# adaLN's row products tied to TensorE's weight chunks, in the recurrence and in the down sweeps

## The chip, the cores and the metric

The kernel runs on one core of a Trainium2 chip. Five engines work side by side, each through its own instructions in order: TensorE (PE; its weight loads are listed as PEld), VectorE (DVE), ScalarE (ACT), GpSimd (POOL) and SyncE (SP), whose queue issues the DMAs here. The metric is the device time of one execution in microseconds, as the median of several runs.

## The reference

One decoder block for 512 tokens of width 2048 in float32. An adaLN vector comes from `c` and modulates every sub-layer: two shifts, two scales, two gates, each 2048 long. Cut to what matters:

```python
c_act = silu(c)                                   # 1 x 2048
mod = c_act @ w_ada + b_ada                       # 1 x 12288
sh1, sc1, gt1, sh2, sc2, gt2 = split(mod, 6)
h = rmsnorm(x, norm1_g) * (1 + sc1) + sh1
p = h @ w_in                                      # 2048 -> 4384
mix = concat(rwkv7(p[:3360]), pool(p[3360:])) @ w_out
x = x + gt1 * mix
h = rmsnorm(x, norm2_g) * (1 + sc2) + sh2
x = x + gt2 * (conv_ffn(h) @ w_down)              # 5632 -> 2048
out = rmsnorm(x, norm_f_g)
```

`rwkv7` is a recurrence over the tokens for 16 heads of width 64; `pool` takes moving means over 2, 4, 8 and 16 tokens.

## The kernel before, in words

Everything is laid out with features on the 128 partitions and the 512 tokens along the free axis. A planner (the tile framework) lays out each engine's order of instructions ahead of time: it takes instructions in the order of their priority (the order in which they are written down, unless a block raises it) as soon as its own clock says that their inputs and buffers are there. On the chip each engine then runs its list strictly in that order and waits on semaphores. Buffers of one tag are handed out in the order in which their tiles are written down.

**Projections.** `project` takes the weights in chunks of 128 x 512 (four 128 x 128 blocks): `split_weights` loads a chunk into `wraw` (four buffers, L113), ScalarE rounds it to `whi` (L115), VectorE takes the rest `wlo` (L117; three buffers each), and `mm3` issues three matmuls a block (L121 to L123), twelve a chunk.

**adaLN's rows.** `mod` has 96 columns of 128 values. Each is a row product: a slice of w_ada is loaded with 128 rows on the partitions, and one VectorE instruction multiplies it by the broadcast `silu(c)` and sums it up (`scalar_tensor_tensor` with `accum_out`, followed by a short read of the accumulator). The first 32 (1024 KB each, L196) are made in the first stage. The next 48 are cut into halves of 1024 elements, 96 rows of 512 KB, in `ada_rest` (L364 to L373, tile `war`, two buffers, broadcast `cq`, results in `modq`). The last 16, the gates of the down projection, are cut into quarters of 512 elements, 64 rows of 256 KB, in `ada_gate2` (L1079 to L1085, tile `wa` under tag t1, broadcast `cb2` under tag t0, two buffers each, results in `modg`).

**The recurrence** (L711 to L742) goes through four groups of four heads. `front` and `rest` of a group are written under a raised priority (`hp`); in `rest` a scan of eight steps (L607 to L636) goes back and forth between TensorE, VectorE (L612, L634) and ScalarE (`ua`, L617). Under groups 0 to 2 the projections of the next group's heads run as filler: `win_some`, six tiles of four chunks, 24 chunks a group. The pool heads are done there too; their weights (`load_pw`, L295) share the two buffers of tag `war` with the rows. `ada_rest(24 * g, 24 * g + 24)` is written at the end of each of groups 0 to 2, at plain priority. Under group 3 and behind it runs most of the output projection, `project(ps, a["wout"][f, :, 0 : NM * P], M)` for ten tiles `f`, 40 chunks (L758 to L767), and `ada_rest(72, 96)` is written behind that (L768). The stage that follows loads x back (L854) and uses `mod[:, 48:80]` in its norm.

**The down sweeps.** `actd` holds 44 tiles of the activated up-projection. The first sweep (L1088 to L1101) goes through them in 11 groups of DK = 4: `act_tiles` loads and splits four (L1064, L143, L144), then `down` runs one weight chunk for each of the NB = 8 output tiles, which sum up in eight banks: 88 chunks. The second sweep (L1104 to L1109) does the other eight output tiles over nine groups, 72 chunks; the last two groups of it are done in token halves behind that. In the first sweep, groups 1 to 8 have eight rows each in front of their chunks:

```python
if 1 <= n <= 8:
    ada_gate2((n - 1) // 2, range(8 * ((n - 1) % 2), 8 * ((n - 1) % 2) + 8))
```

Group 9 adds up the quarters into `mod[:, 80:96]`. The gates are used when the last group of the first sweep goes through `residual`, and in L1109 at the end of the second.

Of the kernel before, what the change touches and what calls it, by code (L numbers as in the profile page):

```python
# [1 line left out]

# [1 line left out]

# [5 lines left out]
F32 = mybir.dt.float32  # L10
# [3 lines left out]
ALU = mybir.AluOpType  # L14
PSUM = bass.MemoryType.PSUM

P = 128
T = 512
D = 2048
KT = D // P  # L20
NF = 44
# [7 lines left out]
NB = 8  # L29
# [5 lines left out]
DK = 4  # L35
# [27 lines left out]
def block_kernel(ctx, tc, a, out, stop=None, dbg=None):  # L63
    nc = tc.nc
    V, S, G, PE = nc.vector, nc.scalar, nc.gpsimd, nc.tensor
# [23 lines left out]
    def cols(name, lo, hi):  # L89
        return vec[:, COLS[name] + lo : COLS[name] + hi]  # L90
# [11 lines left out]
    mod = cp.tile([P, 96], F32, tag="mod", name="mod")  # L102
# [3 lines left out]
    V.tensor_scalar_add(b1p, cols("b_ada", 16, 32), 1.0)  # L106

    mark = [None, None]

    def split_weights(src, eng=V):  # L110
        w = src.shape[-1]
        raw = wp.tile([P, WC], F32, tag="wraw", name="wraw", bufs=4)
        nc.sync.dma_start(raw[:, 0:w], src)  # L113
        hi = wp.tile([P, WC], F32R, tag="whi", name="whi", bufs=3)
        mark[0] = S.copy(hi[:, 0:w], raw[:, 0:w]).ins  # L115
        lo = wp.tile([P, WC], F32R, tag="wlo", name="wlo", bufs=3)
        mark[1] = eng.tensor_tensor(lo[:, 0:w], raw[:, 0:w], hi[:, 0:w].bitcast(F32), op=ALU.subtract).ins  # L117
        return hi, lo

    def mm3(ps, wh, wl, xh, xl, start, stop):  # L120
        PE.matmul(ps, wh, xh, start=start, stop=False)  # L121
        PE.matmul(ps, wh, xl, start=False, stop=False)  # L122
        return PE.matmul(ps, wl, xh, start=False, stop=stop)  # L123

    def project(ps, src, acts, start=True, stop=True, engs=(V,)):

        n = len(acts)
        for k0 in range(0, n, WC // P):
            nk = min(WC // P, n - k0)
            wh, wl = split_weights(src[:, k0 * P : (k0 + nk) * P], engs[k0 // 4 % len(engs)])  # L130
            for kk in range(nk):
                k = k0 + kk
                sl = slice(kk * P, (kk + 1) * P)
                last = mm3(ps, wh[:, sl], wl[:, sl], *acts[k], start=start and k == 0, stop=stop and k == n - 1)
        return last

    def slots(k, tag="a"):
        return (actp.tile([P, T], F32R, tag=f"{tag}h{k}", name=f"{tag}h{k}"),
                actp.tile([P, T], F32R, tag=f"{tag}l{k}", name=f"{tag}l{k}"))
# [32 lines left out]
    cact = tc.dram_tile([1, D], F32, name="cact")  # L172
# [6 lines left out]
    if True:  # L179
        cb = p0.tile([P, D], F32, tag="cb", name="cb")  # L180
# [29 lines left out]
        for k in range(KT):  # L210
# [7 lines left out]
            hi, lo = slots(k)  # L218
# [26 lines left out]
        for k in range(KT):  # L245
# [3 lines left out]
            hi, lo = slots(k)  # L249
# [111 lines left out]
    cq = [None]  # L361
    modq = ra.tile([P, 2, 48], F32, tag="modq", name="modq")

    def ada_rest(n0, n1):  # L364
        for n in range(n0, n1):
            kq, j = divmod(n, 48)
            if j == 0:
                cq[0] = ra.tile([P, 2 * T], F32, tag="cq", name="cq")
                nc.sync.dma_start(cq[0], cact[0:1, kq * 2 * T : (kq + 1) * 2 * T].partition_broadcast(P))
            wa = ra.tile([P, 2 * T], F32, tag="war", name="war", bufs=2)  # L370
            nc.sync.dma_start(wa, a["ada2"][kq, j, :, :])
            V.scalar_tensor_tensor(wa, wa, 1.0, cq[0], op0=ALU.mult, op1=ALU.mult,  # L372
                                   accum_out=modq[:, kq, j : j + 1])  # L373

    def slab(t):
        return t[:, 0 : 2 * T].rearrange("p (x c t) -> p x c t", x=2, c=NK)
# [308 lines left out]
                last_mix.append(split_act(NM + x, two(rs)[:, x, :]))  # L685

    sp, last_mix = {}, []

    def win_some(pairs, which):
        for p, i in [(p, i) for p in pairs for i in which]:  # L690
            ps = win_tile(3 + 3 * p + i)
            t = ra.tile([P, T], F32, tag="spill", name="spill", bufs=2)
            shift(ps, 8 * i + p, t)
            d = tc.dram_tile([P, T], F32, name=f"sp{p}_{i}")
            nc.sync.dma_start(d, t)
            sp[p, i] = d

    def hp():
        return tc.high_priority(offset=100000)

    shift(win_tile(8), 17, two(rkv0[2])[:, 1, :])
    def load_cells(g, names):
        got = []
        for i in names:
            t = cell(RKV[i], RKV[i].lower())
            for x in range(2):
                nc.sync.dma_start(two(t)[:, x, :], sp[2 * g + x, i])
            got.append(t)
        return got

    UNDER = {0: POOLS[0:1], 1: POOLS[1:2], 2: POOLS[2:4]}  # L711
    rkv = rkv0
    with hp():
        fr, norm = front(0, rkv)
    for g in range(NQ):
        pairs = (2 * g + 2, 2 * g + 3)
        with hp():
            quad = rest(g, rkv, fr)
            next(quad)
        if g < NQ - 1:  # L720
            win_some(pairs, (1,))
        with tc.high_priority(offset=50000):
            for gi in UNDER.get(g, ()):
                pool(gi)
        if g < NQ - 1:
            win_some(pairs, (0, 2))
            with tc.high_priority(offset=50000):
                r, k = load_cells(g + 1, (0, 1))
        with hp():
            next(quad)  # L730
        if g < NQ - 1:
            with tc.high_priority(offset=50000):
                fr, norm = front(g + 1, (r, k, None))
        with hp():
            next(quad, None)
            if g < NQ - 1:
                rkv = [r, k] + load_cells(g + 1, (2,))
        if g < NQ - 1:
            ada_rest(24 * g, 24 * g + 24)
        if g == 2:  # L740
            V.tensor_add(mod[:, 32:48], modq[:, 0, 0:16], modq[:, 1, 0:16])
            V.tensor_add(mod[:, 32:48], mod[:, 32:48], cols("b_ada", 32, 48))  # L742
# [15 lines left out]
    for f in range(NW):  # L758
# [7 lines left out]
        nc.sync.dma_start(d, xt[:, f % 2, :])  # L766
        part.append(d)  # L767
    ada_rest(72, 96)  # L768
    V.tensor_add(mod[:, 48:80], modq[:, 0, 16:48], modq[:, 1, 16:48])
    V.tensor_add(mod[:, 48:80], mod[:, 48:80], cols("b_ada", 48, 80))  # L770
# [8 lines left out]
    rb = ctx.enter_context(tc.tile_pool(name="rb", bufs=1, reuse_waits="tile"))  # L779
# [26 lines left out]
    def residual(f, ps, gate, acc, lo, hi, fresh):  # L806

        V.scalar_tensor_tensor(x2[f][:, lo:hi], ps, gate, x2[f][:, lo:hi], op0=ALU.mult, op1=ALU.add)
        sumsq(acc, x2[f][:, lo:hi], lo, hi, fresh)
# [121 lines left out]
    at = 0  # L931
    for j in range(2, NORD):
        tiles = []
        for i in range(2):
            ps = bank()
            last = project(ps, a["wup"][2 * j + i - 4, :, :], H2)
# [78 lines left out]
    for n in range(NST):  # L1015
# [12 lines left out]
        t1, t2, t3, t4 = ([TK[k][i] for k in ks] for i in range(4))  # L1028
# [29 lines left out]
    def gate(f):  # L1058
        return mod[:, 80 + f : 81 + f]

    def act_tiles(k0):
        got = []
        for k in range(k0, k0 + DK):
            t = wp.tile([P, WC], F32, tag="wraw", name="ald", bufs=4)  # L1064
            nc.sync.dma_start(t, actd[k])
            got.append(split_act(k % KT, t))
        return got

    def down(ps, f, k0, n, acts, start, stop):
        project(ps, a["wdn"][f, :, k0 * P : (k0 + n) * P], acts, start=start, stop=stop)  # L1070
# [5 lines left out]

    modg = cp.tile([P, 4, KT], F32, tag="modg", name="modg")

    def ada_gate2(kq, js):  # L1079
        cb = rb.tile([P, T], F32, tag="t0", name="cb2", bufs=2)  # L1080
        nc.sync.dma_start(cb, cact[0:1, kq * T : (kq + 1) * T].partition_broadcast(P))
        for j in js:
            wa = rb.tile([P, T], F32, tag="t1", name="wa3", bufs=2)
            nc.sync.dma_start(wa, a["ada3"][kq, j, :, :])
            V.scalar_tensor_tensor(wa, wa, 1.0, cb, op0=ALU.mult, op1=ALU.mult, accum_out=modg[:, kq, j : j + 1])  # L1085

    pss = [bank() for _ in range(NB)]
    for k0 in range(0, NF, DK):  # L1088
        A = act_tiles(k0)
        n = k0 // DK  # L1090
        if 1 <= n <= 8:
            ada_gate2((n - 1) // 2, range(8 * ((n - 1) % 2), 8 * ((n - 1) % 2) + 8))
        if n == 9:
            V.tensor_add(modg[:, 0, :], modg[:, 0, :], modg[:, 1, :])
            V.tensor_add(modg[:, 2, :], modg[:, 2, :], modg[:, 3, :])
            V.tensor_add(modg[:, 0, :], modg[:, 0, :], modg[:, 2, :])
            V.tensor_add(mod[:, 80:96], modg[:, 0, :], cols("b_ada", 80, 96))
        for f in range(NB):
            down(pss[f], f, k0, DK, A, k0 == 0, k0 + DK == NF)
            if k0 + DK == NF:  # L1100
                residual(f, pss[f], gate(f), acc, 0, T, f == 0)  # L1101
    pss = [bank() for _ in range(NB)]
    KL = NF - 2 * DK
    for k0 in range(0, KL, DK):  # L1104
        A = act_tiles(k0)
        for f in range(NB):
            down(pss[f], NB + f, k0, DK, A, k0 == 0, k0 + DK == KL)
            if k0 + DK == KL:
                V.scalar_tensor_tensor(x2[NB + f], pss[f], gate(NB + f), x2[NB + f], op0=ALU.mult, op1=ALU.add)  # L1109
    A = act_tiles(KL) + act_tiles(KL + DK)  # L1110
    for hf in range(2):
        for n in range(NB):
            f = NB + n
# [121 lines left out]
```

## Time and profile before

| | |
|---|---|
| median of 3 runs | 2365.94 us (2362.83 to 2372.0) |
| the profiled execution | 2367.17 us, its span 2365.4 us |
| granted TensorE clock, mean | 0.979 |
| PE busy | 2224.0 us, 94% |
| PEld busy | 1883.8 us, 80% |
| DVE busy | 1512.8 us, 64% |
| ACT busy | 924.0 us, 39% |
| POOL busy | 404.7 us, 17% |
| the 96 rows of L372 | 117.2 us of DVE, 1222 ns each, first at 196.3 us, last at 738.5 us |
| the 64 rows of L1085 | 43.8 us of DVE, 690 ns each, first at 1860.7 us, last at 2004.6 us |

The span runs from the first to the last instruction; the time of an execution has a little more around it. In a row of a view, a group of instructions has its line, engine, operation, output and inputs, shapes and count; then the busy time and the mean length of one, then the engine's idle time in front of them and what ended it. `DVE war L372 <- DMA war<-ada` in the table of waits means that VectorE stood idle in front of instructions of L372 until the DMA into `war` had landed; the numbers are the total, the count and the longest. A matmul's recorded length overlaps the next one's, so matmuls are best counted by window. Windows give, for each engine, busy time and count, and then the granted TensorE clock (1.00 is full), the mean busy share of the 16 DMA engines and GB/s.

### The profile page before, as it was taken

The numbers are of one execution on the slowest core, as the hardware profiler recorded it, in microseconds if no ns is written. First come the engines' busy times: TensorE is split into PE (matmuls) and PEld (weight loads), VectorE is DVE, ScalarE is ACT, GpSimd is POOL, SyncE is SP. The second block draws the span as 40 slices with busy tenths as digits, with TensorE's granted clock in tenths as the row PEclk, the third lists the DMA queues.
The fourth block names the chain that finished last, engine by engine and source line by source line (L and its number), as shares of the span: only waits on it lengthen the run. The fifth ranks groups of instructions, "written<-read, shape, count | busy, mean of one in ns | idle before, by whom it ended". The sixth has DMA issues, their size and how long they took to land.

```text
span 2365.4 us, 41904 instructions
## 1 busy us (share of the span) xinstructions
PE 2224.0 (94%) x16306; PEld 1883.8 (80%) x16306; DVE 1512.8 (64%) x2532; ACT 924.0 (39%) x1551; POOL 404.7 (17%) x390
## 2 busy tenths in 40 slices
PE   7998888898979899999999999999999998999997
PEld 5776656665656798889999999999999766888886
DVE  7897667576876469766566666665666555353357
ACT  4335233242423255544434444444444322343333
POOL 0000000000000005643443343433342000000000
PEclk9999999999989999999999999999999999999998
DMA  9885555636775575533333333333334877555555
GB/s 349 301 305 170 157 188 164 205 117 206 226 225 163 179 225 169 148 115 109 116 121 115 113 121 108 116 116 113 109 115 133 272 242 231 148 152 143 143 164 179
DMA packets 197466, 401.42 MB, mean 170 GB/s; under 512 B 37521, under 2 KB 49553, under 8 KB 193041
## 3 DMA queue, kind: packets, MB, share of 16 engines
q1 hardware_dynamic: 197266, 398.73, 53.1%
q8 instruction: 128, 2.10, 0.4%
q14 instruction: 72, 0.59, 0.1%
HBM read 364.56 MB, written 34.09 MB: 169 GB/s over the span
## 4 chain that ended last, share of the span: by engine, by line
PE 48%; DMA 5%; DVE 2%; issue 1%; ACT 0%; SPq 0%; DVEq 0%; ACTq 0%
PE b L123 16%; PE b L121 16%; PE b L122 16%; DMA wa<-ada 2%; DMA ald<-actd 2%; DMA wraw<-wdn 1%; DVE wlo L117 1%; DVE wa L1085 0%; DVE x L1074 0%; DMA x<-x2d 0%; ACT ah L143 0%; DVE al L144 0%; ACT whi L115 0%; SPq L1054 0%; PE b L170 0%
## 5 line engine op out<-in xcount | busy, mean ns | idle before, releaser
L115 ACT CAST whi<-wraw 128x512 fp32r<-128x512 f32 (+1 forms) x594 | 360.1, 609 | 827.8 <-DMA wraw<-wup 264.6
L117 DVE TENSOR_TENSOR wlo<-wraw,whi 128x512 fp32r<-128x512 f32 (+1 forms) x578 | 406.0, 705 | 248.3 <-ACT whi L115 239.9
L123 PE MATMUL b<-ah,wlo 128*128 128x512 f32 (+1 forms) x980 | 352.6, 360 | 16.9 <-DVE wlo L117 15.9
L121 PE MATMUL b<-ah,whi 128*128 128x512 f32 (+1 forms) x980 | 351.3, 358 | 9.4 <-ACT whi L115 8.4
L122 PE MATMUL b<-al,whi 128*128 128x512 f32 (+1 forms) x980 | 349.5, 357 | 0.0
L123 PE MATMUL b<-hh,wlo 128*128 128x512 f32 (+1 forms) x640 | 237.4, 371 | 5.5 <-DVE wlo L117 5.4
L121 PE MATMUL b<-hh,whi 128*128 128x512 f32 (+1 forms) x640 | 237.7, 371 | 0.0
L122 PE MATMUL b<-hl,whi 128*128 128x512 f32 (+1 forms) x640 | 237.2, 371 | 0.0
L123 PEld LDWEIGHTS b<-ah,wlo 128*128 128x128 f32 x980 | 186.6, 190 | 53.2 <-DVE wlo L117 26.6
L121 PEld LDWEIGHTS b<-ah,whi 128*128 128x128 f32 x980 | 186.6, 190 | 38.6 <-ACT whi L115 13.7
L122 PEld LDWEIGHTS b<-al,whi 128*128 128x128 f32 x980 | 186.5, 190 | 26.4
L969 DVE TENSOR_TENSOR pl<-raw,ph 128x768 fp32r<-128x768 f32 x104 | 102.9, 989 | 153.6 <-ACT ph L968 153.6
L123 PE MATMUL mm<-ah,wlo 128*128 128x512 f32 x444 | 186.6, 421 | 6.6 <-DVE wlo L117 6.6
L121 PE MATMUL mm<-ah,whi 128*128 128x512 f32 x444 | 185.5, 418 | 7.2 <-ACT whi L115 6.6
L122 PE MATMUL mm<-al,whi 128*128 128x512 f32 x444 | 183.8, 414 | 0.0
L957 POOL TENSOR_TENSOR sums<-sums,raw 128x256 f32<-128x256 f32 x104 | 107.6, 1034 | 416.1 <-DVE sl L969 410.2
L123 PE MATMUL b<-tk,sl 128*128 128x256 f32 x624 | 176.7, 283 | 0.5 <-DVE sl L969 0.5
L122 PE MATMUL b<-tk,sh 128*128 128x256 f32 x624 | 176.6, 283 | 0.0
L121 PE MATMUL b<-tk,sh 128*128 128x256 f32 x624 | 176.1, 282 | 0.0
L372 DVE SCALAR_TENSOR_TENSOR war<-war,cq 128x1024 f32<-128x1024 f32 x96 | 117.2, 1222 | 85.5 <-DMA war<-ada 85.1
L968 ACT CAST ph<-raw 128x768 fp32r<-128x768 f32 x104 | 86.4, 831 | 164.4 <-PE b L122 157.8
L956 POOL TENSOR_TENSOR sums<-raw 128x512 f32<-128x512 f32 x104 | 137.7, 1324 | 67.9 <-DMA raw<-wups 36.3
(277 smaller groups left out, 4711.1 us busy)
## 6 DMA issues: line engine op xcount, KB each, us to landing
raw<-wups SPq DMA_DIRECT2D x104, 512.0 KB, 3.5
war<-ada SPq DMA_DIRECT2D x96, 512.0 KB, 4.3
wraw<-wdn SPq DMA_DIRECT2D x192, 256.0 KB, 3.1
wraw<-wup SPq DMA_DIRECT2D x160, 256.0 KB, 3.6
wa<-ada SPq DMA_DIRECT2D x32, 1024.0 KB, 7.7
wraw<-win SPq DMA_DIRECT2D x108, 256.0 KB, 4.1
ald<-actd SPq DMA_DIRECT2D x88, 256.0 KB, 2.8
wraw<-wout SPq DMA_DIRECT2D x78, 256.0 KB, 4.0
```

The lines of the kernel that those rows point to most:

```text
L115: mark[0] = S.copy(hi[:, 0:w], raw[:, 0:w]).ins
L117: mark[1] = eng.tensor_tensor(lo[:, 0:w], raw[:, 0:w], hi[:, 0:w].bitcast(F32), op=ALU.subtract).ins
L121: PE.matmul(ps, wh, xh, start=start, stop=False)
L122: PE.matmul(ps, wh, xl, start=False, stop=False)
L123: return PE.matmul(ps, wl, xh, start=False, stop=stop)
L372: V.scalar_tensor_tensor(wa, wa, 1.0, cq[0], op0=ALU.mult, op1=ALU.mult, accum_out=modq[:, kq, j : j + 1])
L956: G.tensor_tensor(sa, raw[:, 1:3, :], raw[:, 0:1, :].to_broadcast([P, 2, W2]), op=ALU.add)
L957: G.tensor_tensor(sb2[:, 0, :], sa[:, 0, :], raw[:, 2, :], op=ALU.add)
L968: act = S.copy(hi[:, sl, :], t)
L969: dve = V.tensor_tensor(lo[:, sl, :], t, hi[:, sl, :].bitcast(F32), op=ALU.subtract)
```

## The change

`project` notes the last matmul of each chunk in a list, `beats`. `in_step(op, beat)` tells the planner to place `op` behind that matmul in its order; it is an edge without a semaphore, so nothing waits for it on the chip. In `ada_rest` each row is tied to a beat among those noted since the last call: 24 rows to 24 chunks in groups 0 to 2, and 24 rows to 40 chunks for the last call.

For the gates, `ada_gate2` becomes a generator that issues the loads and keeps one more row loaded than it hands out. `gate_step` is called behind each chunk of both down sweeps and does one row behind every second chunk from the seventh on, tied to that chunk's beat. The rows of the first eight gates come first (32 rows, up to chunk 68), then those of the other eight (up to chunk 132); each half is added up on its own. The row's own instruction, its tiles, its DMAs and their sizes stay as they are. The number of DMAs is the same: 64 rows and eight of `cb2`.

```diff
@@ block_kernel
+    beats = []
+
+    def in_step(op, beat):
+        tc.add_manual_dep(op.ins, beat.name, mybir.DependencyInfo(mybir.DependencyClass.NoSync,
+                                                                  mybir.DependencyReason.DATA), reason="pace")
@@ project
                 last = mm3(ps, wh[:, sl], wl[:, sl], *acts[k], start=start and k == 0, stop=stop and k == n - 1)
+            beats.append(last.ins)
         return last
@@ ada_rest
     def ada_rest(n0, n1):
+        b, at = len(beats) - first_beat[0], first_beat[0]
         for n in range(n0, n1):
...
-            V.scalar_tensor_tensor(wa, wa, 1.0, cq[0], op0=ALU.mult, op1=ALU.mult,
-                                   accum_out=modq[:, kq, j : j + 1])
+            op = V.scalar_tensor_tensor(wa, wa, 1.0, cq[0], op0=ALU.mult, op1=ALU.mult,
+                                        accum_out=modq[:, kq, j : j + 1])
+            i = at + (n - n0) * b // (n1 - n0)
+            if i < len(beats):
+                in_step(op, beats[i])
+        first_beat[0] = len(beats)
@@ ahead of front(0, rkv)
+    first_beat[0] = len(beats)
@@ the gates
-    def ada_gate2(kq, js):
...
+    def ada_gate2(js):
+        loaded = []
+        for kq in range(4):
+            cb = rb.tile([P, T], F32, tag="t0", name="cb2", bufs=2)
+            nc.sync.dma_start(cb, cact[0:1, kq * T : (kq + 1) * T].partition_broadcast(P))
+            for j in js:
+                wa = rb.tile([P, T], F32, tag="t1", name="wa3", bufs=2)
+                nc.sync.dma_start(wa, a["ada3"][kq, j, :, :])
+                loaded.append((wa, cb, modg[:, kq, j : j + 1]))
+                if len(loaded) == 2:
+                    yield loaded.pop(0)
+        yield loaded.pop(0)
+
+    rows = itertools.chain(ada_gate2(range(NB)), ada_gate2(range(NB, KT)))
+
+    def gate_step(n):
+        if n % 2 or n < 6:
+            return
+        row = next(rows, None)
+        if row:
+            wa, cb, got = row
+            in_step(V.scalar_tensor_tensor(wa, wa, 1.0, cb, op0=ALU.mult, op1=ALU.mult, accum_out=got), beats[-1])
+        done = (n - 4) // 2
+        if done in (4 * NB, 4 * KT):
+            lo = done // 4 - NB
...
@@ first sweep
         A = act_tiles(k0)
-        n = k0 // DK
-        if 1 <= n <= 8:
-            ada_gate2((n - 1) // 2, range(8 * ((n - 1) % 2), 8 * ((n - 1) % 2) + 8))
-        if n == 9:
...
         for f in range(NB):
             down(pss[f], f, k0, DK, A, k0 == 0, k0 + DK == NF)
+            gate_step(k0 // DK * NB + f)
@@ second sweep
             down(pss[f], NB + f, k0, DK, A, k0 == 0, k0 + DK == KL)
+            gate_step((NF + k0) // DK * NB + f)
```

More of the change, by code (lines that the diff above doesn't have):

```diff
@@ L1 @@
 from contextlib import ExitStack
+import itertools
 import numpy as np
@@ L687, in block_kernel @@
     sp, last_mix = {}, []
+    first_beat = [0]
     def win_some(pairs, which):
@@ L1077, in block_kernel @@
     modg = cp.tile([P, 4, KT], F32, tag="modg", name="modg")
-    def ada_gate2(kq, js):
[L1080 to L1085, printed above, removed]
+    def ada_gate2(js):
[21 more added lines that the diff above has]
+            lo = done // 4 - NB
+            r = slice(lo, lo + NB)
+            V.tensor_add(modg[:, 0, r], modg[:, 0, r], modg[:, 1, r])
+            V.tensor_add(modg[:, 2, r], modg[:, 2, r], modg[:, 3, r])
+            V.tensor_add(modg[:, 0, r], modg[:, 0, r], modg[:, 2, r])
+            V.tensor_add(mod[:, 80 + lo : 80 + lo + NB], modg[:, 0, r], cols("b_ada", 80 + lo, 80 + lo + NB))
     pss = [bank() for _ in range(NB)]
@@ L1089, in block_kernel @@
         A = act_tiles(k0)
-        n = k0 // DK
-        if 1 <= n <= 8:
-            ada_gate2((n - 1) // 2, range(8 * ((n - 1) % 2), 8 * ((n - 1) % 2) + 8))
-        if n == 9:
[L1094 to L1097, printed above, removed]
         for f in range(NB):
             down(pss[f], f, k0, DK, A, k0 == 0, k0 + DK == NF)
+            gate_step(k0 // DK * NB + f)
             if k0 + DK == NF:
```

## The prediction

> **What bounds the kernel now.** I read the page's part 1 first, then the table of waits, then windows stage by stage, because the rows that the change moves stand in two stages only: the recurrence (196 to 748 us) and the first down sweep (1853 to 2051 us).
>
> ```profile
> PE 2224.0 (94%) x16306; PEld 1883.8 (80%) x16306; DVE 1512.8 (64%) x2532; ACT 924.0 (39%) x1551; POOL 404.7 (17%) x390
> DVE war L372 <- DMA war<-ada: 85.1, 54, 6.2
> DVE wa L1085 <- DMA wa<-ada: 45.1, 38, 3.5
> L372 DVE SCALAR_TENSOR_TENSOR war<-war,cq 128x1024 f32<-128x1024 f32 x96 | 117.2, 1222 | 85.5 <-DMA war<-ada 85.1
> ```
>
> TensorE is busy 94% of the span, so a gain has to come out of its remaining gaps, or out of time in which it issues slowly. The two waits say what adaLN's rows do on VectorE: it stands idle 85.1 us in front of the 96 rows of L372 and 45.1 us in front of the 64 rows of L1085, each time because the row's own DMA has not landed. VectorE takes its instructions in order, so what stands behind such a row waits too. Two short timelines of VectorE show it, first in the recurrence, then in the down sweep:
>
> ```profile
> 427.01 1.23 DVE L372 SCALAR_TENSOR_TENSOR war<-war,cq 128x1024 f32<-128x1024 f32 x1 [6.16 <-DMA war<-ada]
> 428.16 0.08 DVE L372 DVE_READ_ACCUMULATOR war<-war,cq 128x1 f32 x1
> 428.16 1.22 DVE L586 TENSOR_TENSOR X<-X,bt 128x1024 f32<-128x1024 f32 x1
> ...
> 1938.86 0.69 DVE L1085 SCALAR_TENSOR_TENSOR wa<-wa,cb 128x512 f32<-128x512 f32 x1 [3.45 <-DMA wa<-ada]
> 1939.48 0.08 DVE L1085 DVE_READ_ACCUMULATOR wa<-wa,cb 128x1 f32 x1
> 1939.48 0.69 DVE L117 TENSOR_TENSOR wlo<-wraw,whi 128x512 fp32r<-128x512 f32 x1
> ```
>
> At 428.16 the addition to X, on which the recurrence's next matmuls wait, starts in the moment in which a row is done for which VectorE had idled 6.16 us. At 1939.48 it is the split of a weight chunk.
>
> **The down sweeps, term by term.** Windows of equal length, columns busy time and count by engine, then granted clock, DMA share, GB/s: the stretch with the rows, and the one behind it without.
>
> ```profile
> 1877.00:2029.50 152.50, 138.31 (x578) 106.10 (x578) 84.36 (x188) 43.49 (x73) 0.00 (x0) 1.00 0.73 231
> 2029.50:2182.00 152.50, 152.50 (x674) 126.34 (x673) 67.68 (x100) 56.28 (x93) 0.00 (x0) 1.00 0.51 145
> ```
>
> Same kind of matmul, same clock, 578 against 674 in 152.5 us. One takes 152.5 / 674 = 0.2263 us when nothing holds it up, so the 96 that are missing cost 96 x 0.2263 = 21.7 us. That is all the rows can cost there. After the change there is a row (0.69 + 0.08 us of VectorE) per two chunks, which is 2 x 12 x 0.2263 = 5.4 us of TensorE, and VectorE is busy 67.68 of 152.5 us in the rowless stretch; 28 rows more there make it 67.7 + 28 x 0.77 = 89 of 152.5. How long a row's DMA takes stands in the list of DMA issues (size, median time from issue to landing), for the recurrence's rows and for the sweep's:
>
> ```profile
> war<-ada SPq DMA_DIRECT2D x96, 512.0 KB, 4.3
> wa<-ada SPq DMA_DIRECT2D x64, 256.0 KB, 3.6
> ```
>
> In the sweep a row is loaded at least one row ahead, so 5.4 us of lead stand against 3.6 us. The DMAs are as many as before (64 rows, 8 of cb2); 23 of the rows (behind chunks 88 to 132) move into the second sweep, where the DMA share is 0.51 and not 0.73. On SP's queue such an issue still waits for the VectorE row that frees the buffer, with weight loads queued behind it, but these run four buffers ahead. The extra additions (8 of 8 columns instead of 4 of 16) are short, and the gates are due 12 and 20 chunks after them. I take 20 us off, leaving 1.7 us for splits that a row delays. Ends: 21.7 us off if no row is felt; nothing off if the DMAs stay late. If the cover goes, the first to be late is the weight split L117, as now.
>
> **The recurrence.** The four groups end their scans with the eighth `ua` (L617). Windows between the scans, with the first scan and the rest behind the last one (same columns):
>
> ```profile
> 196.00:307.40 111.40, 92.28 (x1052) 68.65 (x1052) 80.17 (x134) 41.87 (x60) 0.95 (x1) 0.91 0.53 159
> 307.40:336.00 28.60, 27.54 (x421) 17.32 (x422) 19.13 (x44) 9.77 (x27) 0.00 (x0) 1.00 0.69 222
> 336.00:441.50 105.50, 88.84 (x1093) 65.53 (x1086) 72.09 (x122) 36.08 (x51) 0.95 (x1) 0.92 0.57 170
> 471.00:568.70 97.70, 88.09 (x1127) 64.08 (x1119) 64.81 (x108) 37.63 (x53) 0.95 (x1) 0.98 0.47 141
> 603.50:716.80 113.30, 92.17 (x1119) 69.26 (x1110) 87.07 (x147) 41.48 (x61) 0.95 (x1) 0.89 0.71 222
> 747.80:813.00 65.20, 64.26 (x356) 51.99 (x345) 24.88 (x39) 19.49 (x35) 0.00 (x0) 1.00 0.38 115
> ```
>
> And VectorE's time in L372 alone, by stretch; a row counts twice there (itself and the read of its sum):
>
> ```profile
> 196.00:307.40 111.40, 22.16 (x36) 0.91 0.53 159
> 307.40:336.00 28.60, 9.84 (x16) 1.00 0.69 222
> 336.00:441.50 105.50, 18.43 (x30) 0.92 0.57 170
> 441.50:471.00 29.50, 8.62 (x14) 1.00 0.63 201
> 471.00:568.70 97.70, 6.99 (x11) 0.98 0.47 141
> 568.70:603.50 34.80, 13.91 (x24) 1.00 0.76 250
> 603.50:716.80 113.30, 27.34 (x45) 0.89 0.71 222
> 716.80:747.80 31.00, 10.61 (x18) 1.00 0.61 191
> ```
>
> What a row costs now. Between the scans, the stretch with 5.5 rows takes 97.7 us and the one with 15 rows 105.5 us: 7.8 / 9.5 = 0.82 us a row. In the scans, two steps without any row give the bare pace:
>
> ```profile
> 464.30:471.00 6.70, 0.00 (x0) 1.00 0.25 79
> 464.41 0.27 ACT L617 COPY ua<-ch 128x128 f32<-128x128 f32 x1 [0.97 <-PE ch L616]
> 471.05 0.27 ACT L617 COPY ua<-ch 128x128 f32<-128x128 f32 x1
> ```
>
> Two steps in 6.64 us, so seven steps need 23.2 us; the four scans take 28.6 + 29.5 + 34.8 + 31.0 = 123.9 us, 31 us more, over 36 rows: 0.86 us a row. With 0.84 us for all 96 the rows cost about 81 us. A row holds VectorE 1.22 + 0.08 us and idles it 85.1 / 96 = 0.89 us more, 2.2 us in all, so some 0.4 of that time lands on the chain.
>
> What the change leaves. Row by row the paces are: 24 weight chunks in each of groups 0 to 2, a row each; 40 chunks of wout for the last 24 rows. A chunk is 12 matmuls, 2.7 us if TensorE does nothing else and about twice that in a group, while a row's DMA lands in 4.3 us, so most rows find their data. One place stays: the rows share the two buffers `war` with the pool weights, in the order in which they are written down. SP's queue shows both pool weights of group 2 taken together and no row until they are free:
>
> ```profile
> 452.35 0.33 SPq L371 DMA_DIRECT2D war<-ada  x1
> 455.94 2.51 SPq L298 DMA_DIRECT2D pw<-poolw  x2
> 548.34 2.89 SPq L371 DMA_DIRECT2D war<-ada  x2
> ```
>
> So group 2's rows cannot begin before 548 us whatever they are tied to, I estimate eight to be overdue by then (a third of the group's 24 chunks), and they run as closely as their DMAs allow, as now. For these and a few others I leave 20 of the 85.1 us of idling. The last group's rows move: now all are done by 748 us, afterwards those whose chunks run behind the scan land in 748 to 813 us, where VectorE is busy 24.88 of 65.2 us, and cost nothing; 64 us of TensorE are some 20 of the 40 chunks, so 10 rows at least. The 86 others cost 0.4 x 1.30 = 0.52 us each, 45 us, and the idling left 0.4 x 20 = 8 us: 53 us against 81, 28 us less. Not all of it is gained. Under group 3's recurrence TensorE has wout to do, and what is not done there is done behind it; of the 15 us that its stretch gives (31 rows at 0.84 against about 20 at 0.52 and a few us of idling) I count half. Gain: 28 - 7 = 21 us.
>
> Ends of this term. The most: TensorE's idle and half-clock time, (window less busy) + busy x (1 - clock), is 27.4, 23.8 and 31.2 us in the windows that start at 196, 336 and 603.5 us and 11.4 in the 97.7 us from 471, where few rows are; brought to that rate the three give 14.4 + 11.5 + 17.9 = 44 us, and the scans at bare pace 31: 75 us. The least lies below zero: the 86 rows each on the chain with their whole 1.30 us are 112 us against 81, 31 us more. I take the middle because few places change where the rows meet the chain, only how long VectorE idles there. The Trainium skill's page "TensorE: Matmul & The Clock Gate" (Part 1: The HAM clock gate) says the array's clock halves after one idle window of about 3.4 us and needs as long to come back; the trace agrees in kind, 0.89 to 0.92 where TensorE idles most, 1.00 in the down sweep where it idles in short pieces. By that rule the windows from 336 and 603.5 us would give 0.06 x 88.8 + 0.09 x 92.2 = 13.6 us from the clock alone if they came to the 0.98 of the one from 471, and the sum would stand at 2311; by the rows it stays, since 0.84 us a row was measured as a whole, clock and all.
>
> The hand-over behind wout: the last rows now end about when the last chunk does. SP's next loads are those of x:
>
> ```profile
> 808.88 0.33 SPq L113 DMA_DIRECT2D wraw<-wout  x1
> 813.22 1.80 SPq L854 DMA_DIRECT2D x<-part  x4
> ```
>
> Chunk 38 of 40 is split before 813 us, its row takes 1.30 us, so these loads aren't held; were rows left over, each would hold them some 2 us (4.3 us of DMA over two buffers). Nothing for it.
>
> **Sum.** The profiled execution took 2367.2 us for a span of 2365.4, and stands 1.2 us above the median of the runs, 2365.9. 2367.2 - 20 - 21 = 2326.2, on the median's footing 2325.
>
> **The rivals.** (a) Only the sweeps pay: the planner puts the rows into the same VectorE gaps of the recurrence, as the group 2 queue shows it must in part: 2365.9 - 20 = 2346. For it: TensorE is busy 27.54 of 28.6 us in a scan already. (b) The recurrence pays far more: rows that find their data hide in VectorE's gaps and cost a third, 27 of 81 us, less 7 in group 3: 47 + 20 off, 2299. For it: the stretch from 471 us, where TensorE loses least, is the one with fewest rows. (c) Slower: a row directly behind a chunk stands just ahead of the next split or the chain's next step, and each of the 86 costs its whole 1.30 us: 31 - 20 gives 2377. It decides from (81 + 20) / 86 = 1.17 us a row. For it: at the start of a group VectorE is full already,
>
> ```profile
> 356.00:376.00 20.00, 15.38 (x237) 12.43 (x240) 19.81 (x25) 8.40 (x13) 0.00 (x0) 1.00 0.59 185
> ```
>
> 19.81 of 20 us with one row in it; against it: there is nearly no idling to add there and the planner ranks rows last. (d) The change doesn't do what it says: the order is laid out by the planner's clock, no wait holds a row behind its chunk on the chip, and the DMAs stay late, 85 and 45 us of idling: 2366. The Trainium skill's "Perfetto Trace Analysis" (Identifying the Most-Contended Engine) would have the engine with the highest occupancy mended first, and by it bubbles on a VectorE at 64% would not move the end; the 96 missing matmuls speak against that.
>
> **How the numbers follow.** Forecast 0.51, (a) 0.22, (b) 0.11, (c) 0.07, (d) 0.09. The forecast's own range is 2308 to 2338. What a measurement can tell from no change is about 0.5%, 12 us. Faster: forecast, (b) and nearly all of (a), 0.82; same: (d) and a little of (a), 0.11; slower 0.07. The range for 8 in 10 takes in (a) and most of (b): 2297 to 2354.
>
> **What would show it.** L1085's successor idles VectorE under 5 us for its DMA, and windows of 152.5 us in the first sweep hold some 670 matmuls. In the recurrence the wait for `war` falls to about 20 us, most of it behind 548 us less the gain, scans take 25 to 27 us, and the last rows stand behind the last scan. Wrong I would be if that wait stays above 50 us, if scans stay at 29 us or more, or if the loads of x wait for a row.

## The result, and the profile after

The changed kernel takes 2332.2 us (median of 5, 2323.1 to 2332.7) where the kernel before takes 2365.9: ratio 0.9836, 95% interval 0.9813 to 0.986. The forecast was 2325 us, with 2308 to 2338 as its own range. The profiled execution took 2332.65 us for a span of 2330.9, against 2365.4 before: 34.5 us.

The page's part 1 of the changed kernel, and from its table of waits the line for the rows of the recurrence (L381 now, L372 before; the last column is the longest wait):

```profile
PE 2202.7 (95%) x16306; PEld 1878.0 (81%) x16306; DVE 1512.6 (65%) x2536; ACT 925.9 (40%) x1551; POOL 403.3 (17%) x390
DVE war L381 <- DMA war<-ada: 47.2, 35, 5.0
```

VectorE does the same work as before and idles 47.2 us in front of the rows instead of 85.1. For the gates' rows (L1115, L1085 before) there is no such line any more: none of the 64 waits for its DMA. The first sweep, in windows of the length used before (busy time and count of PE, PEld, DVE, ACT, POOL; clock, DMA share, GB/s), both now with rows in them:

```profile
1864.00:2016.50 152.50, 152.50 (x675) 126.27 (x674) 74.59 (x142) 51.38 (x84) 0.00 (x0) 1.00 0.66 199
2016.50:2169.00 152.50, 152.50 (x675) 126.27 (x673) 83.59 (x159) 56.37 (x92) 0.00 (x0) 1.00 0.66 199
```

675 matmuls in 152.5 us, where 578 stood beside the rows before and 674 without them: the whole 21.7 us are back. What TensorE lost there before shows in its own waits, here in the window of the 578 (1877 to 2029.5 us):

```profile
PE b L123 <- DVE wlo L117: 11.5, 15, 1.5
```

In the two windows of the changed kernel TensorE waits for no split at all. One place shows why: a row (L1115) now lies between two splits (L124, L117 before) that wait for ScalarE, and costs none of them anything.

```profile
1900.35 0.69 DVE L124 TENSOR_TENSOR wlo<-wraw,whi 128x512 fp32r<-128x512 f32 x1 [2.03 <-ACT whi L122]
1900.96 0.69 DVE L1115 SCALAR_TENSOR_TENSOR wa<-wa,cb 128x512 f32<-128x512 f32 x1
1901.57 0.08 DVE L1115 DVE_READ_ACCUMULATOR wa<-wa,cb 128x1 f32 x1
1903.07 0.69 DVE L124 TENSOR_TENSOR wlo<-wraw,whi 128x512 fp32r<-128x512 f32 x1 [1.42 <-ACT whi L122]
```

The recurrence, in windows cut at the starts and ends of its four scans as before, the last one from the fourth scan's end to the first load of x:

```profile
196.00:299.00 103.00, 85.64 (x1049) 63.88 (x1047) 71.50 (x119) 41.29 (x59) 0.95 (x1) 0.97 0.47 138
299.00:325.20 26.20, 25.38 (x400) 15.74 (x404) 15.13 (x38) 10.24 (x28) 0.00 (x0) 1.00 0.57 181
325.20:428.40 103.20, 87.55 (x1122) 65.05 (x1113) 76.01 (x129) 36.70 (x52) 0.95 (x1) 0.97 0.62 188
428.40:453.50 25.10, 24.68 (x387) 15.19 (x390) 12.82 (x34) 8.93 (x25) 0.00 (x0) 1.00 0.54 173
453.50:561.70 108.20, 93.59 (x1138) 67.48 (x1129) 78.81 (x132) 38.37 (x55) 0.95 (x1) 0.96 0.61 182
561.70:589.70 28.00, 27.69 (x403) 17.23 (x407) 16.98 (x41) 10.34 (x28) 0.00 (x0) 0.93 0.63 193
589.70:696.90 107.20, 86.30 (x1103) 66.55 (x1096) 77.63 (x133) 41.47 (x62) 0.95 (x1) 0.89 0.61 194
696.90:721.70 24.80, 24.57 (x410) 15.31 (x414) 13.45 (x35) 8.72 (x26) 0.00 (x0) 1.00 0.49 143
721.70:798.70 77.00, 74.13 (x378) 60.02 (x371) 46.57 (x79) 21.79 (x39) 0.00 (x0) 1.00 0.68 221
```

The scans take 26.2 + 25.1 + 28.0 + 24.8 = 104.1 us where they took 123.9. Between scans, group 2's stretch became longer, 108.2 against 97.7 us: it was nearly free of rows and now has 16. The third scan ends at 589.7 us (603.5 before, 13.8 us earlier), the fourth at 721.7 (747.8, 26.1 us earlier), and the loads of x, which close the stage, are issued at 798.7 us (813.2, 14.5 us earlier). So the last group won 12.3 us on the chain, and nearly none of it arrived at the loads of x. The two stages' gains, 14.5 and 21.7 us, make up the 34.5 us but for 1.7 us lost between them.

### The profile page after: what moved, and what is told of

It is laid out like the page before. It is cut to its first block, busy times and chain, and to the rows that moved or that the text cites. A ratio compares the mean times of both kernels' runs of the same rounds, so it can differ in the third digit from the quotient of the medians.

```text
span 2330.9 us, 41813 instructions
## 1 busy us (share of the span) xinstructions
PE 2202.7 (95%) x16306; PEld 1878.0 (81%) x16306; DVE 1512.6 (65%) x2536; ACT 925.9 (40%) x1551; POOL 403.3 (17%) x390
## 4 chain that ended last, share of the span: by engine, by line
PE 60%; DVE 2%; DMA 2%; ACT 0%; issue 0%; SPq 0%; DVEq 0%; ACTq 0%
PE b L130 20%; PE b L128 20%; PE b L129 20%; DVE wlo L124 1%; DMA wraw<-wdn 1%; DMA wraw<-wout 1%; DVE hl L159 0%; DVE x L1089 0%; ACT whi L122 0%; DVE acc L819 0%; DMA ald<-actd 0%; DVE h L157 0%; DMA x<-part 0%; DMA x<-x2d 0%; DVE x L823 0%
## 5 line engine op out<-in xcount | busy, mean ns | idle before, releaser
L124 DVE TENSOR_TENSOR wlo<-wraw,whi 128x512 fp32r<-128x512 f32 (+1 forms) x578 | 406.5, 705 | 270.9 <-ACT whi L122 263.1
L381 DVE SCALAR_TENSOR_TENSOR war<-war,cq 128x1024 f32<-128x1024 f32 x96 | 116.9, 1220 | 47.3 <-DMA war<-ada 47.2
```

The source lines that it names most:

```text
L381: op = V.scalar_tensor_tensor(wa, wa, 1.0, cq[0], op0=ALU.mult, op1=ALU.mult, accum_out=modq[:, kq, j : j + 1])
```

## Experiments

The ratios are against the kernel before on the same chip. One measure beside the time is steadier than it: the first load of x, which closes the recurrence's stage with wout. Among four kernels whose recurrence is the same (the changed one and three below) it stands at 794.0, 794.2, 796.5 and 798.7 us, 795.9 in the mean; in the kernel before and one with its recurrence at 813.2 and 816.3, 814.8 in the mean. So one execution's stage is known to some 3 us, and the recurrence's gain is nearer 19 us than the 14.5 us of the one pair of profiles. Every stage time below is that of one profiled execution, which need not be the median one.

| kernel | median us, ratio [95% interval] | fourth scan ends | first load of x | matmuls in 152.5 us, first sweep |
|---|---|---|---|---|
| before | 2365.9 | 747.8 | 813.2 | 578 |
| changed | 2332.2, 0.9836 [0.9813, 0.986] | 721.7 | 798.7 | 675 |
| rec_only | 2348.7, 0.9934 [0.9908, 0.9959] | 714.7 | 794.0 | 581 |
| sweep_only | 2348.2, 0.9931 [0.9904, 0.9958] | 750.9 | 816.3 | 674 |
| no_rows | 2275.8, 0.9632 [0.9605, 0.9659] | 668.9 | 739.6 | |
| rows_nodma | 2302.4, 0.9742 [0.9711, 0.9772] | 691.4 | 766.1 | |
| load_nowait | 2318.6, 0.9791 [0.9771, 0.9812] | 701.7 | 781.4 | |
| own_pw | 2321.3, 0.9804 [0.9783, 0.9824] | 717.4 | 795.3 | |
| shift_late | 2347.9, 0.9927 [0.9898, 0.9955] | 709.6 | 814.2 | |
| shift20 | 2333.8, 0.9866 [0.9847, 0.9886] | 714.5 | 803.0 | |
| shift20_own | 2331.9, 0.9849 [0.9835, 0.9864] | 708.1 | 797.9 | |
| tie_groups | 2336.6, 0.9872 [0.9854, 0.9889] | 730.4 | 800.1 | |
| gate_2per | 2348.8, 0.9922 [0.9902, 0.9943] | 717.6 | 796.5 | 593 |
| gate_1per | 2325.9, 0.9831 [0.9812, 0.9849] | 717.2 | 794.2 | 675 |

### The two parts alone

`rec_only` has the gates' code of before:

```diff
-    def gate_step(n): ...
+        if 1 <= n <= 8:
+            ada_gate2((n - 1) // 2, range(8 * ((n - 1) % 2), 8 * ((n - 1) % 2) + 8))
```

> The changed kernel with the gates' rows put back into the first sweep in bursts of eight; only the recurrence's rows keep their places behind chunks. Theory 1 (the two parts add up, each with its own mechanism): the sweep loses its 21.6 us again, the recurrence keeps its 14.5 us, so about 2332 + 21 = 2353 us, and the end of wout stands at 795 us as in the changed kernel. Rival (the sweep gains because the recurrence now hands over differently): the first sweep keeps some of its gain, below 2345 us.

`sweep_only` has no tie in the recurrence:

```diff
-            if i < len(beats):
-                in_step(op, beats[i])
```

> The changed kernel without the tie of the recurrence's rows to chunks (they are placed as before); only the gates' rows are spread over both sweeps. Theory 1 (the parts add up): 2366 - 21.6 = 2344 us, every group of eight chunks in the sweeps takes 21.76 us. Rival: it needs the other part too, above 2352 us.

2348.7 and 2348.2 us. The ratios multiply to 0.9866, the changed kernel has 0.9836 with an interval that ends at 0.986: within the noise the parts add up. Each stage shows its own part alone, 581 matmuls against 674 in the sweep, 794.0 against 816.3 us for the load of x. `rec_only` ended lower than expected and `sweep_only` higher, by some 4 us each, as their first loads of x do; the sweep itself is as expected.

### What the rows still cost

`no_rows` leaves the 96 rows of the recurrence out, loads and products:

```diff
     def ada_rest(n0, n1):
+        if n0 == 0:
+            G.memset(modq, 0.0)
+        return
```

> The changed kernel with the recurrence's 96 rows left out altogether, loads and products (their sums are set to zero): what the rows still cost where they stand now. Theory 1 (a row still lands on the chain with some 0.5 us, 86 of them, as the prediction put it, and the idling of 47 us with 0.4 of it): 35 to 55 us less chain, of which TensorE's own work lets 25 to 40 us through, 2292 to 2307 us. Rival (TensorE's work is the bound of the recurrence now and the rows are hidden): less than 12 us, 2320 us or more.

`rows_nodma` keeps the products without their loads:

```diff
-            nc.sync.dma_start(wa, a["ada2"][kq, j, :, :])
-            op = V.scalar_tensor_tensor(wa, wa, 1.0, cq[0], ...)
+            op = V.scalar_tensor_tensor(wa, cq[0], 1.0, cq[0], ...)
```

> The changed kernel with the 96 products kept but their loads left out (each multiplies the broadcast vector by itself), so no row can wait for a DMA and 50 MB less are moved. Theory 1 (what is left of the loss is mostly rows that still find their data late, 47 us of idling, 0.4 of it on the chain): 15 to 20 us less than the changed kernel, about 2315 us. Rival (what is left is the time that the products hold VectorE): less than 6 us, 2327 us or more.

`load_nowait` keeps both, but no product reads what is loaded:

```diff
-            nc.sync.dma_start(wa, a["ada2"][kq, j, :, :])
-            op = V.scalar_tensor_tensor(wa, wa, 1.0, cq[0], op0=ALU.mult, op1=ALU.mult, ...)
+            load = nc.sync.dma_start(wa, a["ada2"][kq, j, :, :])
+            if len(ops) >= 2:
+                in_step(load, ops[-2])
+            op = V.scalar_tensor_tensor(cq[0], cq[0], 1.0, cq[0], op0=ALU.mult, op1=ALU.max, ...)
```

> The changed kernel with all 96 loads of rows still issued (each ordered behind the product two rows before it, as now) but with products that read only the broadcast vector, so that the 50 MB move and no product waits for them: it leaves out w_ada in these products. The run without loads was 30 us faster than the changed kernel. Theory 1 (the waits in front of the products are what costs): as fast as without loads, 2300 to 2307 us. Rival (the traffic costs: it delays other transfers and SP's queue): 2325 us or more. In between, the distance to the two ends gives the shares.

2275.8, 2302.4 and 2318.6 us. Without rows the stage closes 795.9 - 739.6 = 56 us earlier, so the rows cost 56 us after the change and 814.8 - 739.6 = 75 us before it. The rival that TensorE's work already was the bound is out. By the steps between the runs, in the first load of x: 739.6 to 766.1 us is 26 us for the time in which the products hold VectorE; 766.1 to 781.4 is 15 us for the loads themselves, though nothing waits for them; 781.4 to 795.9 is 15 us for what hangs on the products having to wait, each to some 3 us. Neither theory for `load_nowait` was right: loads and waits share evenly. The last step takes away more than the idling of VectorE. In the changed kernel SP's queue waits 121.6 us for products to free the rows' buffers, with other loads behind it; in `load_nowait` it waits 74.0 us for the buffer's earlier load instead. Which of the two makes the 15 us was not tested. That the traffic slows other transfers stands in the list of DMA issues (KB each, median us to landing), first of `rows_nodma`, then of `load_nowait`:

```profile
wraw<-win SPq DMA_DIRECT2D x108, 256.0 KB, 3.4
```

```profile
wraw<-win SPq DMA_DIRECT2D x108, 256.0 KB, 4.3
```

The same weight chunk lands in 3.4 us without the rows' 50 MB and in 4.3 us with them (4.1 us in the changed kernel). What of these 15 us comes from that and what from the issues on SP's queue was not told apart.

### A buffer of their own for the pool weights

```diff
-        t = ra.tile([P, 2 * T], F32, tag="war", name="pw", bufs=2)
+        t = ra.tile([P, 2, P], F32, tag="pw", name="pw")          # one half at a time
```

> The changed kernel with the pool heads' weights in a buffer of their own (in halves of 128 KB, which is what still fits), so that they no longer hold one or both of the rows' two buffers. Theory 1 (held buffers are what makes rows late: at the start of groups 0 and 1 and behind 545 us in group 2): the idling for the rows' DMA falls from 47 us to below 25, the time by some 8 to 14 us, to about 2320 us. Rival (the row's own DMA time of 4.4 us against two buffers is it): idling stays above 38 us, time within 5 us of 2332.

The wait, from the table of waits of `own_pw`:

```profile
DVE war L384 <- DMA war<-ada: 43.8, 29, 7.5
```

43.8 us against 47.2: by the idling it is the rival. Group 2's rows no longer had to wait for the pool weights, and the idling only moved: ahead of 301 us it fell from 13.4 to 5.1 us, from 430 to 600 us it rose from 5.7 to 14.3. The first load of x, 795.3 us, is the others' 795.9. The median of 2321.3 us, though, is what Theory 1 gave and 11 us below the changed kernel's. The intervals of the two ratios overlap, and the profiled execution was the slowest of the four (2329.65 us), so its stages can't show a gain; it is left open whether there is one.

### Where the rows lie

`shift_late` puts 16 rows into each of groups 0 to 2 and 48 behind wout's chunks, `shift20` 20 and 36, `shift20_own` adds the buffer from above; the rows for `mod[:, 32:48]` come first:

```diff
+    ROWS = [(q, j) for q in (0, 1) for j in range(16)] + [(q, j) for q in (1, 0) for j in range(16, 48)]
-            ada_rest(24 * g, 24 * g + 24)
+            ada_rest(16 * g, 16 * g + 16)
-    ada_rest(72, 96)
+    ada_rest(48, 96)
```

> The changed kernel with 16 rows in each of groups 0 to 2 instead of 24 and 48 rows tied to the 40 chunks of wout instead of 24; the rows that are needed first come first. Theory 1 (a row costs some 0.6 us in groups 0 to 2, where the 56 us of the 96 rows lie, and little behind the last scan): 24 rows fewer there, 8 to 14 us faster, about 2321 us. Rival (under group 3 and in wout a row costs the same, or the denser rows run late there): within 5 us of 2332, or slower.

> As the run with 16 rows a group, but 20 rows in each of groups 0 to 2 and 36 tied to the 40 chunks of wout. With 16 a group the third scan ended 18 us earlier than in the changed kernel (0.75 us a row moved), and all was lost again because the last row stood at 818 us, behind wout's last chunk, and the loads of x waited until 814 us. Theory 1 (the price of a row in the groups and the hand-over are two separate things): 12 rows moved give some 8 us, the rows are done before wout's last chunk, the loads of x follow it within 5 us, about 2324 us. Rival (the last rows are late again, since each takes 3.6 us of DMA and buffers there): loads of x held, 2332 us or more.

> The same with the pool heads' weights in a buffer of their own. Theory 1 (the two add up, 8 us and some 3 us by the stages of the profile): about 2321 us. Rival (the own buffer only lets rows into the front of group 2, which was free of them): the same as without it, within 2 us.

2347.9, 2333.8 and 2331.9 us: each time the rival. With 16 rows a group the fourth scan ends at 709.6 us, earlier than in any kernel with the same recurrence as the changed one (714.7 to 721.7), and everything is lost again at the hand-over. SP's queue in `shift_late` (start, length, issues):

```profile
802.49 0.86 SPq L120 DMA_DIRECT2D wraw<-wout  x2
804.99 3.17 SPq L382 DMA_DIRECT2D war<-ada  x2
808.26 0.39 SPq L120 DMA_DIRECT2D wraw<-wout  x1
810.90 3.22 SPq L382 DMA_DIRECT2D war<-ada  x2
814.22 5.49 SPq L871 DMA_DIRECT2D x<-part  x10
```

A load of a row waits on SP's queue for the product two rows before it, the weight loads and the loads of x stand behind it, and the last row is done at 818 us. In `shift20` the last row stands at 801.0 us and the loads of x at 803.0: the rival, "late again". With 24 rows there, as in the change, the last row is done by 793 us and the loads follow wout's own last chunk. With the own buffer the loads of x stand at 797.9 us, and the time is that of the change again. So the stage takes no more rows for nothing: 36 gain nothing over 24, and 48 lose 15 us.

`tie_groups` ties only the 72 rows of groups 0 to 2:

```diff
-            if i < len(beats):
+            if i < len(beats) and n < 72:
```

> The changed kernel with the tie only for the 72 rows of groups 0 to 2; the last 24 are placed as early as the planner can, as before the change. It tells the recurrence's gain of 14.5 us apart. Theory 1 (moving the last rows behind the scan of group 3 gives little at the end of wout, because TensorE has wout to do either way): 0 to 4 us slower than the changed kernel. Rival (the last rows under group 3 are where the gain comes from): 8 us slower or more, about 2340 us.

2336.6 us. The fourth scan ends at 730.4 us, 9 to 16 us later than in the kernels with the tie, and the first load of x at 800.1 us, 4 us behind their mean. By the stage that is Theory 1, at its edge. The time does not decide: it is 4 us above the changed kernel's by the medians and 8.5 us by the ratios, whose intervals just overlap, and the profiled execution was the fastest of the five (2333.5 us). As far as this one profile goes, what the last rows do to group 3's chain arrives at wout's end by a third.

### How densely a sweep can take rows

`gate_2per` does two rows behind each chunk from 6 to 37, `gate_1per` one behind each from 6 to 69:

```diff
-        if n % 2 or n < 6:
+        if n < 6:
             return
-        row = next(rows, None)
-        if row:
+        for row in itertools.islice(rows, 2):      # gate_1per keeps next(rows, None)
```

> The changed kernel with the gates' rows two per chunk behind chunks 6 to 37 of the first sweep, four times as dense as in the changed kernel and about twice as dense as in the kernel before, still one row loaded ahead. Theory 1 (what counts is that a row's DMA of 3.6 us is issued early enough: with two rows in 2.7 us it is not): the sweep loses again, 10 us or more, 2342 us or more. Rival (it was the bursts of eight between the splits, not the rate): less than 4 us lost, below 2337 us.

> The changed kernel with one gate row per chunk behind chunks 6 to 69 of the first sweep, as many rows in as much time as in the kernel before, but evenly and one loaded ahead. Theory 1 (a row's DMA of 3.6 us has some 5.4 us of lead at this rate, two at a chunk had 2.7): no loss against the changed kernel, groups of eight chunks at 21.76 us, within 3 us. Rival (the rate itself, its DMA traffic and VectorE time in the first sweep, is what cost): 8 us or more lost.

2348.8 and 2325.9 us. The wait of the rows, TensorE's wait for splits between 1861 and 2013.5 us and two windows of `gate_2per`, the second ending with its last row:

```profile
DVE wa L1114 <- DMA wa<-ada: 41.2, 40, 2.7
PE b L130 <- DVE wlo L124: 9.7, 16, 1.1
1861.00:2013.50 152.50, 141.45 (x593) 108.85 (x592) 87.95 (x197) 46.05 (x77) 0.00 (x0) 1.00 0.75 234
1861.00:1984.00 123.00, 112.32 (x467) 85.60 (x466) 73.85 (x173) 35.06 (x58) 0.00 (x0) 1.00 0.81 253
```

and of `gate_1per`, in which TensorE waits for no split there:

```profile
DVE wa L1115 <- DMA wa<-ada: 33.2, 25, 3.7
1861.00:2013.50 152.50, 152.50 (x675) 126.27 (x674) 91.31 (x201) 50.38 (x84) 0.00 (x0) 1.00 0.78 250
1861.00:1984.00 123.00, 123.00 (x544) 101.85 (x543) 72.49 (x161) 40.22 (x67) 0.00 (x0) 1.00 0.78 250
```

Both idle VectorE for late rows, 41.2 and 33.2 us; one loses 82 matmuls in the window, 18.6 us, the other none. In the 123 us in which both have rows they move 250 and 253 GB/s and keep VectorE busy 72.49 and 73.85 us, nearly the same, and 77 matmuls stand between them: neither the traffic nor VectorE's busy time is the cause. With one row per chunk, even VectorE's longest wait (3.73 us, for the row at 1980.68 us) makes TensorE wait for no split; with two per chunk, or with a burst of eight as before, the splits come too late. That the splits ahead of TensorE make up for a single late row, and not for a second one before the next split, is read from the order; no run varies how far they are ahead. Theory 1 had the verdict of both runs right, but not the reason: in `gate_1per` the DMAs do come late. Nor is the second sweep needed for the gain.

## Why the prediction was right, point by point

- **The sweeps, 20 us forecast.** 21.7 us in the windows. The term was taken from the count of missing matmuls, and its upper end was the truth: TensorE waits for no split, no row waits for its DMA (under 5 us was expected), some 670 matmuls a window were, 675 came.
- **What the rows cost.** 81 us before and 53 us after, from 0.84 us a row, against 75 and 56 us by the runs without rows. The forecast had split the 53 us into 45 for VectorE's time and 8 for idling; it is 26, 15 for the waits and 15 for the loads themselves, a share that the forecast did not have. That the sums are so near is luck in part. In the scans alone the price is close: 19 rows are left there of 36, and the 104.1 us are 11.3 above the bare pace of 4 x 23.2, so 0.59 us a row against 0.86 before and 0.52 in the forecast.
- **The idling left, 20 us.** 47.2 us: wrong by more than double, just inside the 50 us that I had named as the bound. Group 2's rows did begin about when forecast (545 us against 548), but they idle VectorE only 5.7 us from there to 600 us. The pool weights that hold the rows' buffers are not what the idling hangs on (`own_pw`: 43.8 us), and what it is stays open.
- **Group 3, half of 15 us.** This is the term of the sum that was mis-sized. On the chain its 12.3 us came (26.1 at the fourth scan's end less 13.8 at the third's), but at the first load of x the gain is 14.5 us, so 0.7 us of it arrived and not 8. In the mean over all kernels that share the two recurrences the third scan ends 17.6 us earlier, the fourth 31.6 and the load of x 18.9: 14 us on the chain, 1.3 arrived. TensorE has wout to do under that scan either way. So groups 0 to 2 gave 17.6 us where the forecast had 13, and group 3 1.3 where it had 8; the two misses make each other up, and that is luck. Forecast for the recurrence 21 us, measured 14.5 in the pair of profiles and about 19 over all kernels that share the two recurrences; the distance of 7 us between 2325 and 2332 lies here in that pair, and some 3 us of it are within what one execution differs from another.
- **Scans at 25 to 27 us:** 26.2, 25.1, 28.0, 24.8. The third, with 7 rows in it where the others have 3 to 5, is the slow one, as before.
- **The hand-over, nothing.** Right for 24 rows, and the danger was real: `shift_late` is the mishap that was named ("if the loads of x wait for a row").
- **The rivals.** Only the sweeps pay (a): `rec_only` alone gains 0.66%, out. Far more (b): the 56 us that the rows still cost are there, but this change does not reach them. Slower by rows at full price (c): a row costs 56 / 96 = 0.58 us on the stage, below its 1.30 us of VectorE. Nothing changes (d): out.
- **The clock.** In the stretches that end with a scan's start the granted clock rose from 0.91 and 0.92 to 0.97 and 0.97 in the first two, where TensorE's idle time went from 19.1 and 16.7 to 17.4 and 15.7 us. It fell from 0.98 to 0.96 in the third (9.6 to 14.6 us idle), and stayed at 0.89 in the fourth, where TensorE still idles 20.9 of 107.2 us. So in kind the trace agrees with the rule of the Trainium skill's page "TensorE: Matmul & The Clock Gate" (Part 1: The HAM clock gate), that idle windows halve the clock. The time of 2311 us that the forecast gave by it did not come: the stretch from 589.7 us kept its 0.89.

## What to carry to other kernels

A side job that waits for its own DMA does not cost what the engine idles, but what stands behind it in that engine's order: here 33 us of idling cost nothing with one row per weight chunk, and 41 us cost 18.6 us with two. Price such rows by the consumer's lost issue slots in a window of equal length with and without them, as with 578 against 674 matmuls, and look for a free stretch of the same kernel as the measure. When work is moved out of a chain into filler, count the filler's end and the queue of the next stage's loads, not the chain's end: 12 us won under group 3 became about 1, and 48 rows there instead of 24 held the next loads and lost all.

## What was not expected of the hardware

Loads on which no product waits cost 15 us of the stage. With 50 MB more in 570 us a weight chunk of 256 KB landed in 4.3 us instead of 3.4, and SP's queue waited 74.0 us for earlier loads into the rows' buffers; the shares are open. And the time of the recurrence's stage differs by up to 4.7 us between executions of kernels in which it is the same (first load of x at 794.0 to 798.7 us), while the sweeps agree to a matmul in 675.
